# A one-layer hybrid encoder step: the softmax reciprocals of attention brought to rows by a narrow transposition and spread by two DMA queues

## Chip, cores and metric

One NeuronCore of a Trainium2 chip runs one program. The metric is the device time of one execution in microseconds, as the median of three executions. Beside these times there is one profiled execution with its trace.

## The reference

The reference computes one layer for 2048 prompt tokens and 32 sample tokens, model width 1024. An adaLN-modulated RMSNorm is followed by one wide input projection, two parallel token mixers (sparse attention and a short gated convolution), a merge by sigmoid gates, an output projection and a gated residual. The change lies in the sparse attention of the prompt. Every query keeps 256 keys that an indexer has chosen; this is the part that matters:

```python
s = jnp.einsum('bqhgd,bqkhd->bqhgk', qg, kg).astype(jnp.float32) * (HEAD_DIM ** -0.5)
s = jnp.where(valid[:, :, None, None, :], s, -jnp.inf)
p = jax.nn.softmax(s, axis=-1).astype(v.dtype)
o = jnp.einsum('bqhgk,bqkhd->bqhgd', p, vg)
...
a_out = (o * jax.nn.silu(za)) @ w_pa
```

There are 8 query heads and 2 key heads of dimension 128. Everything is float32.

## The kernel before

The program runs in stages: the normalisation and the token-wise projections with the indexer, the wide projections woven with the choice of the keys, attention, and the output projections. All products of float32 matrices are done as sums of products of split numbers: `split` (line 185) makes a rounded part `hi` on ScalarE and a rest `lo = src - hi` on another engine, by default VectorE, and three matmuls take `hi*hi`, `hi*lo` and `lo*hi`.

**Attention** (function `attention`, line 1216) handles the prompt in 16 blocks of 128 queries, in the order 4, 0, 5, 1, 6, 2, 7, 3, 8 to 15. Block `b` meets `128 * (b + 1)` keys. Each block has four pairs of heads, so there are 64 pairs. The keys that a query does not keep are masked by an additive mask, so the softmax runs over all keys of the block.

`qk(pr)` (line 1307) computes the scores of a pair's two heads, queries on partitions, into the two-bank tiles `ps` (lines 1327 to 1329). VectorE adds the mask and takes the running maximum (line 1338), ScalarE takes the exponential in place and sums it along the row (line 1342), and VectorE computes the reciprocals of the two sums (line 1343). They lie in `sc[:, 20:22]`: one number per query and head, queries on partitions. The weights in the tiles `s` stay unnormalised.

`pv(pr)` (line 1346) transposes the weights on TensorE, two key blocks and two heads at a time, into a bank `pt` (line 1363), splits them into `th` and `tl` (line 1367, in the helper's lines 186 and 187), and accumulates the weighted sum of the values in `po[:, 0:256]` (lines 1371 to 1373): the head dimension is on partitions, the queries of the two heads are along the row. Here the reciprocals are needed along the row and the same on all partitions. The kernel before makes this with matmuls:

- GpSimd rounds the reciprocals into `rr` (line 1352) and takes the rest (line 1353); it multiplies the identity by each, which gives two diagonal matrices for each of the two heads in `dg` (line 1356, two instructions);
- TensorE multiplies a matrix of ones by `dg` twice (lines 1374 and 1375), which leaves the reciprocals on all partitions of `po[:, 256:512]`, the other half of the bank;
- VectorE multiplies the gate `z`, loaded from DRAM (line 1378), by this half (line 1380), and the result by the weighted sum into `a` (line 1381).

Then GpSimd forms three sets of differences of `a` (lines 1383 to 1385), which the output projection's fast multiplication scheme uses, and SyncE stores them to `xa_d` (line 1386). The bank `po` has one buffer, `a` two, `z` three, `dg` two, `th` and `tl` five. `ptile` (line 1233) deals the banks for transpositions in turn, two from one pool and one from another.

**What sets the order.** The loop at line 1410 traces `qk` of a pair and then the `pv` of the pair three before it (`AHEAD = 3`). Between them it traces pieces of `sum_steps` (line 1147): loads, GpSimd additions (lines 376 and 1197) and stores that prepare sums of weights and conv results for the output stage, at a pace set by costs. The order on each engine is then fixed at build time by the tile framework's planner, which works on a modelled timeline (`schedule_with_timeline_sim=True`): an instruction can move ahead of an earlier traced one where the plan finds its inputs and its buffer free. At run time each engine works through its own queue in that order, and waits by semaphores.

SyncE's queue issues nearly all DMAs. GpSimd issues 16 loads of `w_g` at the start of the output stage (line 1555) and the stores of the result (line 1714), ScalarE the stores at line 781 in the first stage.

Of the kernel before, what the change touches and what calls it, by code (L numbers as in the profile page):

```python
# [9 lines left out]
F32 = mybir.dt.float32  # L10
F32R = mybir.dt.float32r
# [91 lines left out]
def body(ctx, tc, x_prompt, x_sample, cache_k, cache_v, cache_idx_k, state_conv, c_prompt, c_sample,  # L103
# [15 lines left out]
    def pad(pool, key):  # L119

        if key not in padded:
            padded.add(key)
            pool.tile([P, 16], F32, name=nm("pad"), tag=nm("pad"))
# [20 lines left out]
    s_d = dp.tile([NF, P, 1024], F32, name="s_d", tag="s_d")  # L144
    o_d = dp.tile([3, 2, 2, P, 4, 512], F32, name="o_d", tag="o_d")
# [7 lines left out]
    ones_r = cp.tile([P, P], F32R, name="ones_r")  # L153
    V.tensor_copy(ones_r, ones)
# [1061 lines left out]
    def attention(shared=None, aside=()):  # L1216
        aside = list(aside)
        sums = []
        with ExitStack() as p2:
# [59 lines left out]
            def block(b):  # L1279
# [65 lines left out]

                def pv(pr):
                    sms, sc = st.pop(pr)
                    po = pso.tile([P, 512], F32, name=nm("po"), tag="pi")
                    g = pr // 2

                    rr = ap_.tile([P, 4], F32R, name=nm("rr"), tag="rr")
                    G.tensor_copy(rr[:, 0:2], sc[:, 20:22])
                    G.tensor_tensor(rr[:, 2:4], sc[:, 20:22], rr[:, 0:2].bitcast(F32), ALU.subtract)
                    dg = ap_.tile([P, 2, 256], F32R, name=nm("dg"), tag="dg")
                    for k in range(2):
                        G.tensor_tensor(dg[:, k, :].rearrange("p (i q) -> p i q", i=2), ident.unsqueeze(1).to_broadcast([P, 2, P]),
                                        rr[:, 2 * k:2 * k + 2].bitcast(F32).unsqueeze(2).to_broadcast([P, 2, P]), ALU.mult)
# [16 lines left out]
                    T.matmul(po[:, 256:512], ones_r, dg[:, 0, :], start=True, stop=False)  # L1374
                    T.matmul(po[:, 256:512], ones_r, dg[:, 1, :], start=False, stop=True)
# [4 lines left out]
                    V.tensor_tensor(z, z, po[:, 256:512], ALU.mult)  # L1380
                    V.tensor_tensor(a[:, 0:256], z, po[:, 0:256], ALU.mult)
                    ps_ = a.rearrange("p (s t) -> p s t", s=8)
# [5 lines left out]
                return prep, [(lambda pr=pr: qk(pr), lambda pr=pr: pv(pr)) for pr in range(4)]  # L1388
# [18 lines left out]
            pend = []  # L1407
            total = sum(c for c, _ in sums)
            did = [0.0, 0.0]
            for nb, b in enumerate(order):  # L1410
# [7 lines left out]
                for qk, pv in blocks[b][1]:  # L1418
                    qk()
                    pend.append(pv)  # L1420
                    if len(pend) > AHEAD:
                        pend.pop(0)()
# [5 lines left out]
            for pv in pend:  # L1428
                pv()
# [454 lines left out]
```

## Time and profile before

| | |
|---|---|
| median of 3 executions | 2855.73 us (2851.65 to 2858.47) |
| profiled execution | 2855.3 us |
| its span, first to last instruction | 2853.4 us |
| granted TensorE clock, mean over the span | 0.994 |
| TensorE, VectorE, ScalarE, GpSimd busy | 97%, 78%, 52%, 34% |
| attention of the prompt, from its first scores to its last weighted sum | about 1780 to 2350 us |
| DMA traffic | 557.19 MB, mean 195 GB/s |

In the rows of the profile, PE is TensorE, PEld its weight loads, DVE VectorE, ACT ScalarE, POOL GpSimd and SP SyncE; a `q` behind the name marks the engine's queue, where DMAs are issued. L1375 is a line of the kernel before. A group's row ends with its busy time and the mean duration of one, and, behind a second bar, with the idle time of the engine just before these instructions and what ended it. In a row by windows, each engine has its busy time and the number of instructions; then come the granted clock, the busy share of the DMA engines and the rate. A row of waits has the total time, the number of waits and the longest. In a row of one source line, the durations are minimum, median and maximum in nanoseconds. A row of DMA issues ends with the median time from issue to landing in microseconds. Matmuls are pipelined, so two of them overlap in the trace.

### The profile page before, as it was taken

To read this page: it belongs to the slowest core of one execution; us is meant where nothing else is said; L and a number is where in the kernel's file an instruction comes from. 1 tells how busy PE (TensorE), PEld (TensorE's weight loads), DVE (VectorE), ACT (ScalarE), POOL (GpSimd) and SP (SyncE) were. 2 spreads that over 40 slices of the span, in tenths; PEclk is the share of its full clock that TensorE was granted. 3 is DMA by queue.
4 is the path that set the end of the run, shared out by engine and by line. 5 is a ranking of instruction groups with operands and counts; after the bars stand their busy time and mean duration, and the time that the engine had idled before them with its cause. 6 is when DMAs were issued, how large, how long until landed. Compare 5 with 4: busy or idle time off the path is not lost. (4 is left out here: it accounts for less than half of the span.)

```text
span 2853.4 us, 53721 instructions
## 1 busy us (share of the span) xinstructions
PE 2768.8 (97%) x18926; PEld 2674.1 (94%) x18926; DVE 2211.7 (78%) x4981; ACT 1486.7 (52%) x2861; POOL 971.3 (34%) x1440
## 2 busy tenths in 40 slices
PE   8999998999999999999999999999999999999998
PEld 6999998999999998999999999889999989999998
DVE  6666576767764778999998777878877768987988
ACT  4434334665545665655554433665655555454453
POOL 3324224545554532322323221576544430010100
PEclk9999999999999999999999999999999999999999
DMA  7425567544554546555576676576555359996785
GB/s 290 165 88 190 170 209 246 191 146 165 167 182 148 168 153 223 184 185 175 181 249 212 204 238 184 146 179 185 149 156 160 113 179 339 279 296 217 249 297 157
DMA packets 462097, 557.19 MB, mean 195 GB/s; under 512 B 171441, under 2 KB 353145, under 8 KB 460793
## 3 DMA queue, kind: packets, MB, share of 16 engines
q1 hardware_dynamic: 452952, 537.33, 59.1%
q0 software_dynamic: 4160, 12.06, 1.2%
q10 hardware_dynamic: 4704, 4.26, 0.4%
q8 instruction: 151, 2.47, 0.4%
q14 instruction: 130, 1.06, 0.1%
HBM read 369.17 MB, written 190.66 MB: 196 GB/s over the span
## 5 line engine op out<-in xcount | busy, mean ns | idle before, releaser
L991 PE MATMUL pm<-bh,wo 128*128 128x352 f32 (+1 forms) x2352 | 755.1, 323 | 6.5 <-ACT ev L1003 4.4
L992 PE MATMUL pm<-bl,wo 128*128 128x352 f32 (+1 forms) x2352 | 756.0, 322 | 0.0
L993 PE MATMUL pm<-bh,wo 128*128 128x352 f32 (+1 forms) x2352 | 754.2, 322 | 0.0
L991 PEld LDWEIGHTS pm<-bh,wo 128*128 128x128 f32 x2352 | 443.3, 189 | 15.1 <-ACT ev L1003 5.7
L992 PEld LDWEIGHTS pm<-bl,wo 128*128 128x128 f32 x2352 | 443.9, 189 | 4.8
L993 PEld LDWEIGHTS pm<-bh,wo 128*128 128x128 f32 x2352 | 442.3, 188 | 4.2 <-issue 0.2
L187 POOL TENSOR_TENSOR wo<-wr,wo 128x512 fp32r<-128x512 f32 x140 | 204.8, 1463 | 597.6 <-ACT wo L186 582.7
L759 PE MATMUL pm<-wh,hhi 128*128 128x256 f32 (+4 forms) x1088 | 307.9, 285 | 5.7 <-DVE sm L733 5.5
L760 PE MATMUL pm<-wl,hhi 128*128 128x256 f32 (+4 forms) x1088 | 307.2, 283 | 2.9 <-DVE wl L187 1.7
L761 PE MATMUL pm<-wh,hlo 128*128 128x256 f32 (+4 forms) x1088 | 305.0, 283 | 0.0
L248 DVE SCALAR_TENSOR_TENSOR sc<-pi,wi,sc 128x512 f32<-128x512 f32 (+3 forms) x287 | 192.2, 670 | 56.7 <-ACT pi L244 53.7
L186 ACT CAST th<-pt 128x512 fp32r<-128x512 f32 (+1 forms) x288 | 155.1, 561 | 137.7 <-PE pt L1363 131.1
L244 ACT ACTIVATE pi<-pi 128x512 f32<-128x512 f32 (+3 forms) x328 | 164.8, 516 | 113.1 <-PE pi L243 112.2
L1459 ACT CAST wh<-rw 128x1024 fp32r<-128x1024 f32 x128 | 134.3, 1052 | 166.0 <-PE ps L1634 81.2
L1633 PE MATMUL ps<-xh,wh 128*128 128x384 f32 (+1 forms) x672 | 214.2, 321 | 2.4 <-ACT wh L1459 0.9
L1634 PE MATMUL ps<-xl,wh 128*128 128x384 f32 (+1 forms) x672 | 214.4, 320 | 0.0
L187 DVE TENSOR_TENSOR tl<-pt,th 128x512 fp32r<-128x512 f32 (+1 forms) x288 | 183.9, 655 | 38.5 <-ACT th L186 37.3
L1635 PE MATMUL ps<-xh,wl 128*128 128x384 f32 (+1 forms) x672 | 211.7, 320 | 0.5 <-DVE wl L1460 0.5
L759 PEld LDWEIGHTS pm<-wh,hhi 128*128 128x128 f32 (+1 forms) x1088 | 198.9, 183 | 8.2 <-issue 3.5
L760 PEld LDWEIGHTS pm<-wl,hhi 128*128 128x128 f32 (+1 forms) x1088 | 199.2, 183 | 4.7 <-POOL wl L187 1.5
L761 PEld LDWEIGHTS pm<-wh,hlo 128*128 128x128 f32 (+1 forms) x1088 | 198.4, 183 | 1.0 <-DVE hlo L187 0.2
L1460 DVE TENSOR_TENSOR wl<-rw,wh 128x1024 fp32r<-128x1024 f32 x128 | 155.3, 1220 | 47.9 <-ACT wh L1459 47.7
(313 smaller groups left out, 7168.6 us busy)
## 6 DMA issues: line engine op xcount, KB each, us to landing
u<-u_d SPq DMA_DIRECT2D x112, 520.0 KB, 4.5
wr<-in_w_f_dram SPq DMA_DIRECT2D x84, 512.0 KB, 3.9
rw<-o_d SPq DMA_DIRECT2D x72, 512.0 KB, 6.8
u_d<-ev SPq DMA_DIRECT2D x168, 176.0 KB, 2.5
rw<-in_w_q_dram SPq DMA_DIRECT2D x56, 512.0 KB, 7.3
wr<-in_w_t_dram SPq DMA_DIRECT2D x32, 512.0 KB, 4.4
xa_d<-a SPq DMA_DIRECT2D x64, 256.0 KB, 3.1
s_d<-ws SPq DMA_DIRECT2D x56, 256.0 KB, 2.8
```

The lines of the kernel that those rows point to most:

```text
L187: (eng or V).tensor_tensor(lo, src, hi.bitcast(F32), ALU.subtract)
L244: S.activation(pi[:n, :w], pi[:n, :w], AF.Relu)
L248: V.scalar_tensor_tensor(sc[:n, o:o + w], pi[:n, :w], wi[:n, b, h:h + 1], sc[:n, o:o + w], ALU.mult, ALU.add)
L759: T.matmul(pm[:n, :ncol], a, hi[:, kt, :ncol], start=(kt == 0), stop=False)
L760: T.matmul(pm[:n, :ncol], a, lo[:, kt, :ncol], start=False, stop=False)
L761: T.matmul(pm[:n, :ncol], b_, hi[:, kt, :ncol], start=False, stop=(kt == KT - 1))
L991: T.matmul(ps[:, :tb], wh[:, kt, :], bh[:, kt, :tb], start=(first and kt == 0), stop=False, **more)
L992: T.matmul(ps[:, :tb], wh[:, kt, :], bl[:, kt, :tb], start=False, stop=False, **more)
L993: T.matmul(ps[:, :tb], wl[:, kt, :], bh[:, kt, :tb], start=False, stop=(kt == 3), **more)
L1633: T.matmul(ps[:, :tb], wh[:, kt, wc], xh[:, kt, :tb], start=(first and kt == 0), stop=False, **more)
L1634: T.matmul(ps[:, :tb], wh[:, kt, wc], xl[:, kt, :tb], start=False, stop=False, **more)
L1635: T.matmul(ps[:, :tb], wl[:, kt, wc], xh[:, kt, :tb], start=False, stop=(kt == 3), **more)
```

## The change

The reciprocals no longer go through diagonal matrices. A new step `spread(pr)` transposes the two columns of reciprocals on TensorE into a `pt` bank (two partitions by 128 columns), ScalarE copies them to the tile `rt` and issues, on its own queue, a DMA that writes them as 1 KB to `r_d` in DRAM. In `pv`, GpSimd issues on its queue a DMA that reads this 1 KB into all 128 partitions of `rb`. VectorE multiplies the gate by the weighted sum in the bank, directly into `a`; GpSimd multiplies `a` by `rb`. `spread` of a pair is traced after the `qk` of the pair two behind it, before the `pv` of the pair ahead of it. The matrix `ones_r`, `rr` and `dg` go; `rt` and `rb` have two buffers each, and a small pad tile stands ahead of `th`.

```diff
+    r_d = dp.tile([NB, 4, 2, P], F32, name="r_d", tag="r_d")
...
-    ones_r = cp.tile([P, P], F32R, name="ones_r")
-    V.tensor_copy(ones_r, ones)
...
+                def spread(pr):
+                    sc = st[pr][1]
+                    pt = ptile()
+                    T.transpose(pt[:2, :P], sc[:, 20:22], ident)
+                    rt = aq.tile([P, P], F32, name=nm("rt"), tag="rt")
+                    S.copy(rt[:2, :], pt[:2, :P])
+                    S.dma_start(r_d[b, pr], rt[:2, :])
+
                 def pv(pr):
-                    sms, sc = st.pop(pr)
+                    sms = st.pop(pr)[0]
                     po = pso.tile([P, 512], F32, name=nm("po"), tag="pi")
                     g = pr // 2
-
-                    rr = ap_.tile([P, 4], F32R, name=nm("rr"), tag="rr")
-                    G.tensor_copy(rr[:, 0:2], sc[:, 20:22])
-                    G.tensor_tensor(rr[:, 2:4], sc[:, 20:22], rr[:, 0:2].bitcast(F32), ALU.subtract)
-                    dg = ap_.tile([P, 2, 256], F32R, name=nm("dg"), tag="dg")
-                    for k in range(2):
-                        G.tensor_tensor(dg[:, k, :].rearrange("p (i q) -> p i q", i=2), ident.unsqueeze(1).to_broadcast([P, 2, P]),
-                                        rr[:, 2 * k:2 * k + 2].bitcast(F32).unsqueeze(2).to_broadcast([P, 2, P]), ALU.mult)
+                    pad(ap_, (id(ap_), "th"), bufs=1)
...
-                    T.matmul(po[:, 256:512], ones_r, dg[:, 0, :], start=True, stop=False)
-                    T.matmul(po[:, 256:512], ones_r, dg[:, 1, :], start=False, stop=True)
...
-                    V.tensor_tensor(z, z, po[:, 256:512], ALU.mult)
                     V.tensor_tensor(a[:, 0:256], z, po[:, 0:256], ALU.mult)
+                    rb = aq.tile([P, 256], F32, name=nm("rb"), tag="rb")
+                    G.dma_start(rb, r_d[b, pr].rearrange("(o i) q -> o (i q)", o=1).broadcast_to([P, 256]))
+                    G.tensor_tensor(a[:, 0:256], a[:, 0:256], rb, ALU.mult)
...
-                for qk, pv in blocks[b][1]:
+                for qk, spread, pv in blocks[b][1]:
                     qk()
                     pend.append(pv)
+                    rows.append(spread)
+                    if len(rows) > AHEAD - 1:
+                        rows.pop(0)()
                     if len(pend) > AHEAD:
                         pend.pop(0)()
...
+            for spread in rows:
+                spread()
             for pv in pend:
                 pv()
```

More of the change, by code (lines that the diff above doesn't have):

```diff
@@ L117, in body, with pad @@
     padded = set()
-    def pad(pool, key):
+    def pad(pool, key, **kw):
         if key not in padded:
             padded.add(key)
-            pool.tile([P, 16], F32, name=nm("pad"), tag=nm("pad"))
+            pool.tile([P, 16], F32, name=nm("pad"), tag=nm("pad"), **kw)
     cp = ctx.enter_context(tc.tile_pool(name="cp", bufs=1))
@@ L1386, in pv @@
                     store(xa_d[pr, :, :, 64 * b:64 * b + 64].rearrange("s p t -> p s t"), ps_)
-                return prep, [(lambda pr=pr: qk(pr), lambda pr=pr: pv(pr)) for pr in range(4)]
+                return prep, [(lambda pr=pr: qk(pr), lambda pr=pr: spread(pr), lambda pr=pr: pv(pr)) for pr in range(4)]
             order = [4, 0, 5, 1, 6, 2, 7, 3, 8, 9, 10, 11, 12, 13, 14, 15]
@@ L1406, in attention @@
                 v_pair(j, vst)
-            pend = []
+            pend, rows = [], []
             total = sum(c for c, _ in sums)
```

## Prediction

> **What bounds the kernel now.** I read the page first, then busy time by stretches of the attention stage, then the waits in that stage, then single instructions.
>
> ```profile
> span 2853.4 us, 53721 instructions
> PE 2768.8 (97%) x18926; PEld 2674.1 (94%) x18926; DVE 2211.7 (78%) x4981; ACT 1486.7 (52%) x2861; POOL 971.3 (34%) x1440
> ```
>
> TensorE is busy for 97% of the span, no other engine for more than 78%. That is an average over stages, so the changed stage has to be read by itself. Its first and its last pair of heads are bounded by the second ones matmul (L1375, 64 of them); the 31st shows where short pairs end.
>
> ```profile
> 1791.95 0.29 PE L1375 MATMUL po<-dg,ones_r 128*128 128x256 f32 x1
> 1956.55 0.28 PE L1375 MATMUL po<-dg,ones_r 128*128 128x256 f32 x1
> 2349.12 0.28 PE L1375 MATMUL po<-dg,ones_r 128*128 128x256 f32 x1
> ```
>
> ```profile
> core 0: us, PE busy (x) PEld busy (x) DVE busy (x) ACT busy (x) POOL busy (x), PEclk, DMA share, GB/s
> 1787.00:1945.00 158.00, 146.88 (x1045) 136.09 (x1044) 125.06 (x390) 95.68 (x217) 101.81 (x279) 0.97 0.64 162
> 1945.00:2350.00 405.00, 397.24 (x2884) 374.53 (x2884) 311.80 (x711) 234.66 (x366) 192.84 (x411) 1.00 0.54 157
> 1787.00:2350.00 563.00, 544.12 (x3927) 510.62 (x3926) 436.86 (x1101) 330.34 (x583) 294.64 (x689) 0.99 0.56 158
> ```
>
> The early stretch has short pairs: 164.6 us between the 1st and the 31st end, 30 intervals of 5.5 us. There TensorE idles 11.1 of 158 us. After 1945 us it idles 7.8 of 405 us. Over the stage it works 544.12 of 563 us, 96.6%, at a granted clock of 0.99. So an instruction less on TensorE is time off the stage, nearly in full, unless something else becomes late. What TensorE does wait for, and what was close to being late:
>
> ```profile
> PEld po L1371 <- ACT th L186: 9.6, 9, 3.6
> PE po L1371 <- DVE a L1381: 5.5, 4, 3.3
> PE po L1371 <- ACT th L186: 2.5, 3, 1.1
> DVE a L1381 <- DMA xa_d<-a: 2.7, 2, 2.5
> POOL dg L1356 <- PE po L1375: 118.6, 39, 11.4
> ```
>
> The waits on ScalarE's cast of the transposed weights sum to 12.1 us (9.6 and 2.5). Four times the next accumulation waited because VectorE had not yet read the bank, and twice VectorE itself was held because the store of tile `a` had not landed. GpSimd's 118.6 us are idle time of an engine that nobody waits for: its `dg` tile had two buffers.
>
> **TensorE.** Removed are the two ones matmuls of each pair, added is one transposition of two columns. Matmuls overlap, so their price is the distance between starts, not the duration.
>
> ```profile
> 2226.32 0.28 PE L1374 MATMUL po<-dg,ones_r 128*128 128x256 f32 x1
> 2226.44 0.28 PE L1375 MATMUL po<-dg,ones_r 128*128 128x256 f32 x1
> 2226.56 0.40 PE L1328 MATMUL ps<-klo,qh 128*128 128x512 f32 x1
> ...
> 2235.50 0.27 PE L1363 MATMUL pt<-ident,s 128*128 128x128 f32 x1
> 2235.52 0.36 PE L1371 MATMUL po<-th,vhi 128*128 128x256 f32 x1
> 2235.72 0.39 PE L1327 MATMUL ps<-khi,qh 128*128 128x512 f32 x1
> ```
>
> Two matmuls take 0.24 us, from 2226.32 to 2226.56: 64 x 0.24 = 15.4 us. A transposition alone among matmuls, with the 256-column matmul behind it, takes 0.22 us (2235.50 to 2235.72); less 0.12 us for that matmul it is 0.10 us. The narrow one streams the same 128 columns of the identity with a narrower weight load, so I take 64 x 0.10 = 6.4 us. Below, it can't be under nothing; above, its whole duration of 0.27 us would make 17.3 us and turn the term round. The spacing is the nearer row, since neighbours hide the rest. Net -9.0 us; times 96.6% for the share in which TensorE is the one that works, **-8.7 us** (bounds -14.9 and +1.8). It waits for the reciprocal of its pair, which is computed two pairs earlier, so I price that wait at nothing; without this cover it would stop every matmul queued behind it, for up to the time of a ScalarE exponential. It also takes a turn of the three banks that the transposed weights use.
>
> **ScalarE.** Added per pair: a copy of the 2x128 result, and the issue of a DMA of 1 KB. Nearest rows: a copy of 128 columns out of the bank, and the DMAs this queue issued elsewhere.
>
> ```profile
> L416 ACT COPY box<-pt x2: 266/267/268, 774.5 to 819.1; 128x128 f32<-128x128 f32 x2
> L781 ACTq DMA_DIRECT2D out_dram<-sm x17: 338/339/414, 217.3 to 462.0; - x17
> ...
> L186 ACT CAST th<-pt 128x512 fp32r<-128x512 f32 (+1 forms) x288 | 155.1, 561 | 137.7 <-PE pt L1363 131.1 <-PE po L1373 3.4 <-DVE tl L187 1.5
> ```
>
> 0.267 + 0.339 = 0.61 us, 64 times 38.8 us. ScalarE goes from 330 to 369 of 563 us. The copy waits for the transposition and the DMA for the copy; behind both stand the next casts and exponentials, and TensorE waits for casts. Scaling its 12.1 us of such waits by 369/330 gives **+1.4 us**. Ends: nothing, if all sits in ScalarE's 233 idle us, and 38.8 us, if every insertion lay ahead of a cast that TensorE awaits; that TensorE waited 12 times for 288 casts speaks for the low end.
>
> **VectorE.** Removed: one of the two multiplications that read the bank.
>
> ```profile
> L1380 DVE TENSOR_TENSOR z<-z,po 128x256 f32<-128x256 f32 x64 | 26.6, 416 | 14.3 <-PE po L1375 13.6 <-DMA xa_d<-a 0.3
> ```
>
> 26.6 us go from an engine that is not the bound. The gain is that the bank comes free 0.416 us sooner; it was waited for four times, at most 4 x 0.42 = 1.7 us. I take **-1.3 us**, since at least once the store, not this read, was late (ends 0 and -5.5).
>
> **GpSimd and the DMAs.** Removed per pair: rounding, difference, two diagonal products. Added: the issue of a DMA that reads 1 KB 128 times (128 KB), and one 128x256 product, ahead of the three differences and the store that were there.
>
> ```profile
> L1352 POOL CAST rr<-sc 128x2 fp32r<-128x2 f32 x64 | 12.0, 187 | 57.6 <-DVE sc L1343 56.7 <-DVE sc L1341 0.5
> L1353 POOL TENSOR_TENSOR rr<-sc,rr 128x2 fp32r<-128x2 f32 x64 | 12.6, 197 | 2.3
> L1356 POOL TENSOR_TENSOR dg<-ident,rr 128x256 fp32r<-128x256 f32 x128 | 76.2, 615 | 120.3 <-PE po L1375 118.6 <-DMA in<-k_d 1.7
> L1197 POOL TENSOR_TENSOR wq<-wq 128x256 f32<-128x256 f32 x96 | 72.3, 760 | 8.8 <-DMA wq<-in_w_q_dram 4.5
> L1383 POOL TENSOR_TENSOR a<-a 128x128 f32<-128x128 f32 x64 | 30.0, 469 | 58.8 <-DVE a L1381 49.1 <-DVE sc L1341 6.1 <-DVE sc L1343 3.4
> L1384 POOL TENSOR_TENSOR a<-a 128x64 f32<-128x64 f32 x64 | 21.1, 329 | 3.5
> L1385 POOL TENSOR_TENSOR a<-a 128x64 f32<-128x64 f32 x64 | 20.8, 325 | 3.7
> L1555 POOL DMA_DIRECT2D x<-in_w_g_dram x16: 548/548/824, 2352.0 to 2422.6; - x16
> z<-z_d SPq DMA_DIRECT2D x64, 128.0 KB, 2.4
> x<-in_w_g_dram POOLq DMA_DIRECT2D x16, 256.0 KB, 5.8
> xa_d<-a SPq DMA_DIRECT2D x64, 256.0 KB, 3.1
> ```
>
> Out go 0.187 + 0.197 + 2 x 0.615 = 1.61 us, in come 0.55 + 0.76 = 1.31 us: 64 x 0.30 = 19 us less work, on an engine with idle time. What matters are two new waits in its queue: the issue waits until the 1 KB has landed in DRAM, and the product until the 128 KB have landed in SBUF. Behind them stand the differences of `a`, its store, the next issue, and the additions of the weight sums, which nothing needs before the output stage. The landing lies between 2.4 us (same bytes, SyncE's queue) and 5.8 us (GpSimd's queue, twice the bytes, heavier traffic).
>
> The Trainium skill, "DMA: Bandwidth & Descriptors", section "Anatomy of one DMA — SWDGE (gpsimd) path", gives such a transfer about 2.0 us plus its bytes over 436 GB/s; by that estimate 128 KB land in 2.3 us. SyncE's 2.4 us agree with it and GpSimd's own 5.8 us do not, so the trace's ends stay; by the page the slow case below would cost nothing.
>
> The transposition is traced two weighted sums and one score product ahead of its use, over 1.5 pair times: 8 us early, 18 us later (33 intervals in 392.6 us, 11.9 us each). Against that stand 0.61 us, a landing of 1 KB (2.4 us), 0.55 us and 2.4 to 5.8 us: 6.0 to 9.4 us. So it is hidden late and about met early. The loop that can stop VectorE, and TensorE behind it, is tile `a` with two buffers: 0.42 (multiply) + 0.76 + 1.12 (differences) + 0.34 (store issue, as ScalarE's) + 3.1 (landing), 5.7 us and the hand-overs for two pairs, so 3 to 3.5 us a pair, under the mean of 5.5. Early pairs vary, so I charge **+2.0 us** (ends 0 and the slow case). The extra 64 x 128 KB = 8.4 MB stand beside 158 GB/s x 563 us = 89 MB, on DMA engines that are busy for 56%; no charge.
>
> **Sum.** -8.7 + 1.4 - 1.3 + 2.0 = -6.6 us. The profiled execution took 2855.3 us, 1.9 us more than its span, and lies 0.4 us under the median of the three runs, 2855.7. Taken from the median: **2849.1 us**. About 0.2%, 5.7 us, is what a measurement can tell from no change, so the forecast stands just past that line, at 2850.0.
>
> **Rivals.**
>
> *A, the forecast* (2841 to 2854): chance 0.62, of which 0.42 below 2850.0. Its low end is -8.7 - 5.5 us with no charge for ScalarE and GpSimd, its high end the sum with B's price.
>
> *B, ScalarE hands the gain back.* One in six insertions delays a cast that TensorE awaits: 38.8/6 = 6.5 us in place of 1.4, and the extra turn of the transposition banks holds large tiles up. Time 2849.1 + 5.1 = 2854, no change. For it: ScalarE's casts are already TensorE's largest wait. Against it: ScalarE stays at 66%. Chance 0.17.
>
> *C, slower: GpSimd's queue sets the pace of the short pairs.* The planner leaves the DMA's issue right before its product, as the code lists it. Then each pair costs GpSimd issue, landing, product and differences in series, 2.43 us plus the landing: 4.8 to 8.2 us, and 6.5 with the middle of 4.1. It decides from 5.5 us on, a landing over 3.1 us: (6.5 - 5.5) x 30 = 30 us, time 2849 + 30 = 2879; with 5.8 us, 81 us and 2930; with 3.1, nothing. For it: the `a` store already held VectorE twice. Against it: the queue orders of this trace start work when its buffer frees (`dg` was waited for 39 times behind the previous pair's matmul), so the issue should stand a pair ahead, and with two buffers the loop product, issue, landing is at most 7.1 us for two pairs, 3.6 us a pair. Chance 0.17.
>
> *D, the change does not do what it says.* The reordered stage loses in its handoffs what the matmuls gave, because the planner fills the freed places otherwise; TensorE's work falls and its idle time grows by as much. Time 2855. Chance 0.04.
>
> **How the numbers follow.** Faster by over 0.2%: 0.42, from A. Within: 0.20 of A, B and D, together 0.41. Slower: 0.17, from C. The range starts at A's low end, 2841, and ends at 2868, beyond B and D and with the part of C in which a landing takes less than 3.7 us.
>
> **What would show it.** Right: TensorE's busy time from 1787 us on falls by some 9 us with its idle time in the stage near 19 us; the narrow transpositions stand 0.10 us apart from their neighbours; ScalarE's waits by TensorE rise by less than 3 us; GpSimd's product waits for its DMA mostly before 1950 us, and VectorE's multiplication rarely for the store. B: more waits of TensorE on casts. C: GpSimd idle before the product in nearly every early pair, VectorE held by the `a` store, and TensorE by VectorE, with the early stretch longer. Wrong would be a changed stage after 1950 us, where nothing but TensorE is near its limit, or a transposition that waits for its reciprocal.

## The result, and the profile after

The changed kernel took 2878.06 us, the median of 6 runs (2874.84 to 2886.08). The kernel before, on the same chip, took 2857.41 us, also the median of 6 (2851.65 to 2858.98). The ratio is 1.0079, with a 95% interval from 1.0063 to 1.0095: slower by 0.8%, where 0.2% faster was forecast. The time lies 10 us above the predicted range.

The page of the kernel after, its first lines:

```profile
span 2874.5 us, 53369 instructions
PE 2774.6 (97%) x18862; PEld 2673.4 (93%) x18862; DVE 2194.8 (76%) x4916; ACT 1499.5 (52%) x2925; POOL 956.9 (33%) x1312
```

The span grew by 21.1 us. VectorE and GpSimd work less, as intended. TensorE has 64 instructions fewer and is busy 5.8 us longer. Busy time by stretches of the attention stage, kernel after, with the columns of the prediction's table. The prediction cut the kernel before at 1787, 1945 and 2350 us; these cuts lie at about the same work (VectorE begins to read the banks of the 1st, 31st and 64th pair into `a` at 1794.3, 1963.6 and 2368.2 us, in the kernel before at 1793.7, 1957.4 and 2350.0):

```profile
1787.00:1948.00 161.00, 144.90 (x989) 129.75 (x989) 113.10 (x351) 97.47 (x238) 92.41 (x207) 0.95 0.74 175
1948.00:2368.00 420.00, 401.29 (x2870) 375.31 (x2869) 305.71 (x680) 245.71 (x408) 189.37 (x353) 0.99 0.60 165
1787.00:2368.00 581.00, 546.19 (x3857) 505.06 (x3857) 418.81 (x1031) 343.18 (x645) 281.77 (x560) 0.98 0.64 168
```

The stage takes 581 us in place of 563, so nearly all of the loss lies in it. TensorE idles 34.8 us (581.00 less 546.19) where it idled 18.9. Most of the increase lies after 1948 us: 18.7 us idle there, against 7.8 us. What TensorE waits for, rows of its waits in the stage, kernel after:

```profile
PE po L1371 <- ACT th L185: 9.7, 6, 4.3
PE po L1372 <- DVE tl L186: 7.0, 18, 1.1
PE pt L1301 <- DMA in<-q_d: 5.5, 3, 4.4
PE pt L1363 <- ACT rt L1350: 3.4, 3, 2.3
PE pt L1348 <- DVE sc L1342: 2.6, 1, 2.6
PE po L1371 <- DVE a L1378: 0.8, 2, 0.6
```

Four things are new. Waits for ScalarE's cast `th` have a longest of 4.3 us, where it was 1.1. A load of `q` that comes late stops TensorE for up to 4.4 us, where the kernel before has this row:

```profile
PE pt L1302 <- DMA in<-q_d: 2.5, 2, 1.3
```

Waits for VectorE's cast `tl` are frequent, 18 where there were 4. And two rows belong to the new step itself: the narrow transposition (L1348) waits for its reciprocal, and the transpositions of the weights (L1363) wait for ScalarE's copy of the narrow one (L1350). One row went the hoped-for way: TensorE waits 0.8 us, not 5.5, for VectorE to read the bank.

**The two longest waits for `th`**, followed back. First TensorE, then ScalarE (two pieces of its timeline), then SyncE's queue, all of the kernel after; the bracket holds the idle time before the instruction and what ended it:

```profile
1932.69 0.58 PE L1371 MATMUL po<-th,vhi 128*128 128x256 f32 x1 [4.33 <-ACT th L185]
1989.06 0.39 PE L1371 MATMUL po<-th,vhi 128*128 128x256 f32 x1 [3.94 <-ACT th L185]
```

```profile
1930.13 0.62 ACT L185 CAST vhi<-in 128x512 fp32r<-128x512 f32 x1 [5.53 <-DMA in<-v_d]
...
1987.90 0.62 ACT L185 CAST vhi<-in 128x512 fp32r<-128x512 f32 x1 [5.59 <-DMA in<-v_d]
1988.43 1.55 ACT L185 CAST th<-pt 128x512 fp32r<-128x512 f32 x3
```

```profile
1918.05 0.46 SPq L1386 DMA_DIRECT2D xa_d<-a  x1
1924.74 0.36 SPq L1159 DMA_DIRECT2D wq<-b_d  x1
1925.15 0.46 SPq L1257 DMA_DIRECT2D in<-k_d  x1
1925.71 0.42 SPq L1257 DMA_DIRECT2D in<-v_d  x1
```

ScalarE was not busy. It stood for 5.5 us ahead of the cast of a block's new values `v`, which had not arrived, and casts of transposed weights stood behind it (three of them at 1988.43). The first of these loads of `v` was issued only at 1925.71 us, because SyncE's queue had stood, after its issue at 1918.05, until 1924.74 ahead of a load for the weight sums (L1159), whose buffer was still being stored. So a late load of a new block stops ScalarE, and ScalarE stops TensorE. The late `q` stops TensorE without ScalarE between, for 4.37 us until 1851.31.

The kernel before had such a chain once. ScalarE, VectorE and TensorE there:

```profile
1918.63 0.62 ACT L186 CAST vhi<-in 128x512 fp32r<-128x512 f32 x1 [5.86 <-DMA in<-v_d]
1919.29 0.69 DVE L187 TENSOR_TENSOR vlo<-in,vhi 128x512 fp32r<-128x512 f32 x1 [4.85 <-ACT vhi L186]
1921.38 0.35 PE L1371 MATMUL po<-th,vhi 128*128 128x256 f32 x1 [3.33 <-DVE a L1381]
```

ScalarE waited for `v`, VectorE's rest of `v` waited for ScalarE, and VectorE's two reads of the bank stood behind that rest; TensorE waited 3.33 us for the second. So a late `v` is not new in kind. New are a second one that reaches TensorE and the later `q`.

Such a stop costs twice. The windows behind the two stalls, and behind a stall of 2.44 us that ended at 2165.09, kernel after, have the granted clock as the third number from the right:

```profile
1932.00:1936.00 4.00, 3.31 (x15) 3.31 (x16) 2.47 (x6) 2.20 (x7) 1.59 (x4) 0.50 0.64 198
...
1989.00:1993.00 4.00, 3.94 (x19) 3.82 (x20) 3.77 (x11) 2.77 (x6) 0.56 (x1) 0.57 1.02 275
...
2165.00:2169.00 4.00, 3.92 (x31) 3.92 (x31) 3.86 (x9) 2.08 (x3) 0.49 (x1) 1.00 0.60 203
```

TensorE works at about half its clock for some 4 us after each of the two, by an estimate from these shares another 2 us each; behind the shorter stall the clock stays at 1.00. The Trainium skill, "TensorE: Matmul & The Clock Gate", section "Part 1: The HAM clock gate (the "warmup" mystery)", says that the clock falls to half after an idle window of about 3.4 us and that busy time of that length releases it. The traces agree for single stalls: 0.50 and 0.57 behind 4.33 and 3.94 us, 1.00 behind 2.44 us. In the kernel before, 3.33 us were enough for 0.57 from 1922 to 1926 us.

**The last pair.** TensorE, kernel after:

```profile
2335.84 0.27 PE L1348 MATMUL pt<-ident,sc 128*2 128x128 f32 x1 [2.59 <-DVE sc L1342]
2335.95 0.60 PE L1363 MATMUL pt<-ident,s 128*128 128x128 f32 x4
2338.84 1.12 PE L1363 MATMUL pt<-ident,s 128*128 128x128 f32 x4 [2.29 <-ACT rt L1350]
```

Behind the last scores, the loop's tail traces the two remaining transpositions at once, ahead of the last three weighted sums. The last one waits for its reciprocal (2.59 us), then the next transpositions wait for ScalarE to have emptied its bank (2.29 us): both behind an exponential over all 2048 keys. From 2340 to 2344 us the granted clock is 0.50 here as well, though neither stall is longer than 2.59 us: two short ones with only five transpositions between them were enough.

### The profile page after: what moved, and what is told of

Read it like the earlier page. It is cut to its first block, busy times and chain, and to the rows that moved or that the text cites. A ratio compares the mean times of both kernels' runs of the same rounds, so it can differ in the third digit from the quotient of the medians.

```text
span 2874.5 us, 53369 instructions
## 1 busy us (share of the span) xinstructions
PE 2774.6 (97%) x18862; PEld 2673.4 (93%) x18862; DVE 2194.8 (76%) x4916; ACT 1499.5 (52%) x2925; POOL 956.9 (33%) x1312
## 3 DMA queue, kind: packets, MB, share of 16 engines
q10 hardware_dynamic: 4960, 4.33, 0.4%
## 4 chain that ended last, share of the span: by engine, by line
PE 66%; DVE 17%; DMA 8%; issue 4%; ACT 3%; POOL 1%; SPq 1%; DVEq 0%; ACTq 0%; POOLq 0%
PE pm L990 8%; PE pm L991 8%; PE pm L992 8%; PE pt L1363 3%; PE pm L759 3%; PE pm L758 3%; PE pm L760 3%; PE ps L1638 2%; PE ps L1639 2%; PE ps L1640 2%; PE po L1372 2%; DMA rw<-in_w_q_dram 2%; PE ps L1326 2%; PE po L1373 2%; PE po L1371 2%
```

## The experiments

Each time is the median of its runs, in microseconds, with the ratio to the kernel before on the same chip; that kernel took 2853 to 2857 us in every series. Line numbers are those of the kernel after. The theories, in the order in which they stood:

- *T1*: what is new on GpSimd holds the loop of tile `a` and through it SyncE's queue, and with it the loads of q, k and v.
- *T2*: waits of the new step have no cover at the last pair.
- *T3*: the planner made a worse order, and none of the added work costs anything by itself.
- *T4*, formed later: the narrow transposition's turn of the three banks is what costs.

| kernel | time | ratio, 95% interval |
|---|---|---|
| after | 2878.1 | 1.0079 [1.0063, 1.0095] |
| no_product | 2878.9 | 1.0092 [1.0071, 1.0113] |
| no_spread | 2856.2 | 1.0009 [0.9997, 1.0021] |
| z_pool | 2899.6 | 1.0158 [1.0137, 1.0178] |
| store_pool | 2868.7 | 1.0058 [1.0037, 1.0078] |
| tail_late | 2867.2 | 1.0055 [1.0036, 1.0074] |
| qkv_act | 2865.4 | 1.0044 [1.0027, 1.0061] |
| qkv_act_before | 2854.3 | 1.0002 [0.9992, 1.0012] |
| tail_qkv | 2859.2 | 1.0021 [1.0010, 1.0032] |
| spread_dve | 2894.7 | 1.0143 [1.0126, 1.0160] |
| before_replan | 2856.8 | 1.0009 [0.9999, 1.0019] |
| rows_dma | 3128.4 | 1.0959 [1.0941, 1.0978] |
| floor | 2838.7 | 0.9958 [0.9939, 0.9976] |
| floor_rows | 2869.2 | 1.0039 [1.0024, 1.0053] |
| floor_rows_qkv | 2852.8 | 1.0003 [0.9991, 1.0015] |
| floor_turn | 2864.3 | 1.0050 [1.0033, 1.0067] |
| floor_rb | 2864.1 | 1.0031 [1.0015, 1.0048] |
| bank_half | 2869.3 | 1.0042 [1.0029, 1.0055] |
| bank_qkv | 2868.9 | 1.0044 [1.0030, 1.0058] |

**Which part costs: product, spread, or the place of the product.** Four kernels, each with one part of the change taken out or moved.

*no_product* drops GpSimd's multiplication.

```diff
-                    G.tensor_tensor(a[:, 0:256], a[:, 0:256], rb, ALU.mult)
```

> The changed kernel without GpSimd's product of a and rb; the rows are still transposed, copied, written and spread, so attention's output stays unnormalised. Before 2857, changed 2878. Theory 1 (the product stands between VectorE's multiplication and the store of a; SyncE's queue waits for that store with the loads of v and q behind it, ScalarE then stands in the cast of v and TensorE idles): the store comes about 0.8 us a pair sooner, SyncE's wait for GpSimd's last difference falls from 87 to about 40 us, time 2855 to 2862. Theory 2 (the spread itself costs: a transposition bank, ScalarE's copy and issue, GpSimd's issue behind the 1 KB write): stays at 2872 to 2880. Theory 3 (no part costs; the planner's new order put the loads of v late by chance): anywhere from 2855 to 2885, without a relation to the part removed.

*no_spread* drops transposition, copy and both DMAs; the product stays, with a constant.

```diff
-                    rows.append(spread)
-                    if len(rows) > AHEAD - 1:
-                        rows.pop(0)()
...
-                    G.dma_start(rb, r_d[b, pr].rearrange("(o i) q -> o (i q)", o=1).broadcast_to([P, 256]))
-                    G.tensor_tensor(a[:, 0:256], a[:, 0:256], rb, ALU.mult)
+                    G.tensor_tensor(a[:, 0:256], a[:, 0:256], ones_w, ALU.mult)
```

> The changed kernel without transposition, copy, 1 KB write and broadcast; GpSimd multiplies a by a constant tile of ones, so the output stays unnormalised. Theory 1: the product still delays the store, 2866 to 2874 (TensorE saves the 6 us of narrow transpositions). Theory 2: 2842 to 2850, that is before less the 15 us of ones matmuls and some stalls. Theory 3: anywhere from 2845 to 2880.

*z_pool* lets GpSimd multiply the gate `z` ahead of the bank instead of `a` behind it.

```diff
+                    G.tensor_tensor(z, z, rb, ALU.mult)
                     a = aq.tile([P, 512], F32, name=nm("a"), tag="a", bufs=2)
                     V.tensor_tensor(a[:, 0:256], z, po[:, 0:256], ALU.mult)
-                    G.tensor_tensor(a[:, 0:256], a[:, 0:256], rb, ALU.mult)
```

> GpSimd multiplies the gate z by rb before the bank is ready, instead of a by rb after it; the result is the same in exact terms and nothing is left out. Theory 1: the tail from the bank to the store is the one of before, 2850 to 2860. Theory 2: 2872 to 2880, as all of the spread is still there. Theory 3: no relation, 2855 to 2885.

*store_pool* issues the store of `a` on GpSimd's queue, so that SyncE's queue never stands for `a`.

```diff
-                    store(xa_d[pr, :, :, 64 * b:64 * b + 64].rearrange("s p t -> p s t"), ps_)
+                    G.dma_start(xa_d[pr, :, :, 64 * b:64 * b + 64].rearrange("s p t -> p s t"), ps_)
```

> The changed kernel with the store of a issued by GpSimd's own queue, behind the differences, instead of SyncE's. Theory 1: SyncE's queue no longer waits for GpSimd, the loads of v are issued in time, 2850 to 2862; GpSimd pays 64 x 0.59 us for the issues, 38 us of an engine that idles. Theory 2: 2872 to 2885. Theory 3: no relation, 2855 to 2885.

Measured: 2878.9, 2856.2, 2899.6 and 2868.7. The first fits T2; the second and the fourth lie between the ranges of T1 and T2, the third above all. Without the product nothing is gained, so T1 in its first form, the product as the cause, falls. Without the spread the whole loss is gone. Moving the product ahead of the bank is worse; the trace has TensorE waiting 18.8 us for `th`, once for 8.1 us, again behind a late `v` (ScalarE waits up to 10.3 us for one). Taking the stores out of SyncE's queue helps, by 9 us (6 by the ratios); a late `q` stops TensorE there too, once for 7.0 us. What GpSimd's product waits for in the kernel after:

```profile
POOL a L1381 <- DVE a L1378: 219.9, 49, 17.5
```

The product waits for VectorE's `a`, 49 times, and none of its waits is ended by the landing of `rb`. The landing (median 3.7 us) was in time, since the issue stands a pair ahead (at 2092.28 us, for instance, for the product at 2109.97).

**Late loads, and the last pair.** *qkv_act* issues the loads of q, k and v on ScalarE's queue, and *qkv_act_before* does the same in the kernel before, as a control. *tail_late* changes only the loop's tail.

```diff
-                load(t.rearrange("p (j c) -> p j c", j=2), d[j * P:(j + 2) * P, :].rearrange("(j p) c -> p j c", p=P))
+                S.dma_start(t.rearrange("p (j c) -> p j c", j=2), d[j * P:(j + 2) * P, :].rearrange("(j p) c -> p j c", p=P))
...
-                            load(q, q_d[r0:r0 + P, 512 * g:512 * g + 512])
+                            S.dma_start(q, q_d[r0:r0 + P, 512 * g:512 * g + 512])
```

> The changed kernel, nothing left out; the loads of q, k and v for the next block are issued by ScalarE's queue instead of SyncE's. Theory 1 in its second form (after the first four runs: not the product, but SyncE's queue as a whole holds these loads behind sums and stores that became later; TensorE's stalls of about 4 us at the starts of blocks are late q, k or v): the stalls of 4.4, 4.3 and 3.9 us at 1851, 1933 and 1989 us go, with the clock loss behind them, 2858 to 2866. Theory 2 (ScalarE's insertions): ScalarE gets 36 more issues of 0.34 us, 2876 to 2885. Theory 3: 2860 to 2885, stalls of the same kind in other places.

> Control: the kernel before with the loads of q, k and v on ScalarE's queue. Theory 1b (late loads are something that the change brought): the kernel before has few such stalls, 2850 to 2858. If moving them is worth as much without the change: 2840 to 2846.

```diff
-            for spread in rows:
-                spread()
-            for pv in pend:
+            for i, pv in enumerate(pend):
+                if i < len(rows):
+                    rows[i]()
                 pv()
```

> The changed kernel, nothing left out; only the last two transpositions of rows move: each is traced ahead of one of the last weighted sums instead of both at once behind the last scores. In the changed kernel's trace TensorE waits there 2.6 us for a reciprocal, 2.3 us for the copy out of the bank and 0.9 us for a cast, and its clock then falls to 0.5 for 4 us. Theory 1 (queue and loads): these are a small part, time 2870 to 2874. Theory 2 (each part of the spread costs where its wait is uncovered): the same 4 to 7 us, with the wait for the reciprocal gone. Theory 3 (plan by chance): 2865 to 2885, waits elsewhere moved too.

*tail_qkv* is both edits in one.

> The changed kernel, nothing left out, with both earlier edits: loads of q, k and v by ScalarE's queue, and the last two transpositions one at a time. Each alone gave 11 to 13 us. Theory 1b and 2 (two separate places): they add up, 2853 to 2858. Theory 3: they do not add up, 2858 to 2872.

Measured: 2865.4, 2854.3, 2867.2 and 2859.2. The same move of the loads that gains 13 us after the change gains nothing before it, so what it gains is a loss that the change made. The waits of TensorE in qkv_act and in tail_late that answer to the rows above, one fence each:

```profile
PE pt L1301 <- DMA in<-q_d: 7.1, 4, 4.7
PE po L1372 <- DVE tl L186: 6.2, 18, 1.1
PE pt L1363 <- ACT rt L1350: 3.1, 2, 2.4
PE po L1371 <- ACT th L185: 2.9, 5, 0.9
PE pt L1348 <- DVE sc L1342: 2.6, 1, 2.6
```

```profile
PE po L1372 <- DVE tl L186: 7.7, 19, 1.5
PE po L1371 <- ACT th L185: 6.5, 5, 2.9
PE pt L1363 <- ACT rt L1350: 1.1, 2, 0.8
```

In qkv_act the waits for `th` are back at 2.9 us, and the two waits of the tail are still there. ScalarE's two waits for `v` of 5.5 and 5.6 us are 2.1 and 1.6 us. The late `q` is not cured: it stops TensorE for 4.7 us here and for 4.9 us in tail_qkv. In tail_late the wait for the reciprocal is gone. Until 2327 us every engine's queue stands there in the same order as in the changed kernel, so only the tail differs; the lower wait for `th` is what one execution differs from another, and the profiled one took 2857.7, 9.5 us under the median.

By the ratios the two edits gain 0.35% and 0.24%, and together 0.58%: they add up. By the medians they gain 12.7 us, as T1 gave it, and 10.9, which is more than the 4 to 7 us that T1 and T2 gave, and together 18.8: 2859.2 lies just past the range for adding up and inside that of T3. T2 is shown, as its edit touches the tail alone. T1 in the form "loads late behind SyncE's queue" has edit, control and waits for it where `v` is concerned. But the planner gave every other engine another order as well, so how much of the gain is the queue alone is not shown. What stays above the kernel before is 0.2%, with the late `q` in it. The waits for `tl` stay in both.

**Other carriers for the step.** *spread_dve* gives the copy to VectorE and the write of 1 KB to GpSimd's queue, *rows_dma* drops transposition and copy and lets a DMA write the reciprocals from their columns to DRAM, 256 elements of 4 bytes.

```diff
-                    S.copy(rt[:2, :], pt[:2, :P])
-                    S.dma_start(r_d[b, pr], rt[:2, :])
+                    V.tensor_copy(rt[:2, :], pt[:2, :P])
+                    G.dma_start(r_d[b, pr], rt[:2, :])
```

> The changed kernel, nothing left out; VectorE instead of ScalarE copies the two rows out of the bank, and GpSimd's queue instead of ScalarE's writes them to DRAM, so ScalarE is as loaded as before. Theory 1: stalls at the starts of blocks stay, 2870 to 2880. Theory 2 (ScalarE's insertions delay casts: TensorE's waits for the rest tl rose from 8 to 19 us): these waits fall back to about 8 us, 2864 to 2872. Theory 3: 2860 to 2885.

```diff
-                    pt = ptile()
-                    T.transpose(pt[:2, :P], sc[:, 20:22], ident)
-                    rt = aq.tile([P, P], F32, name=nm("rt"), tag="rt")
-                    S.copy(rt[:2, :], pt[:2, :P])
-                    S.dma_start(r_d[b, pr], rt[:2, :])
+                    S.dma_start(r_d[b, pr].rearrange("i q -> q i"), sc[:, 20:22])
```

> The changed kernel, nothing left out, but the two columns of reciprocals go to DRAM directly, by a DMA on ScalarE's queue that writes 256 numbers of 4 bytes: no narrow transposition, no turn of a transposition bank, no copy by ScalarE. TensorE's waits for the rest tl were about 12 us in every run with the narrow transposition, also where ScalarE did not copy, and 5 to 6 us in those without. Theory 2b (the transposition's turn of a bank and its waits cost, not the DMAs): these waits fall to 5 to 6 us, the 5 to 6 us at the last pair go, and 6 us of transpositions; 2855 to 2862. Theory 1b (the DMAs and the later stores hold up SyncE's queue and late q, k, v loads remain): 2866 to 2874. Theory 3 (plan by chance): 2850 to 2885 with stalls of q, k, v loads in other places.

Measured: 2894.7 and 3128.4, both above every range. The first has the waits for `tl` no lower (7.2 us), so nothing speaks for the load on ScalarE as their cause; VectorE, which makes `tl`, has the copy instead. Its late loads are worse: TensorE waits 13.3 us for `q`, ScalarE 20.8 us for `v`. The second is worse by far: the DMA of small elements goes with slower transfers beside it, as the last section shows.

**What the removed work was worth, and another traced order.** *floor* is the kernel before without anything that spreads the reciprocals. *before_replan* is the kernel before with the same instructions in another traced order.

```diff
-                    rr = ap_.tile([P, 4], F32R, name=nm("rr"), tag="rr")
...
-                    T.matmul(po[:, 256:512], ones_r, dg[:, 0, :], start=True, stop=False)
-                    T.matmul(po[:, 256:512], ones_r, dg[:, 1, :], start=False, stop=True)
...
-                    V.tensor_tensor(z, z, po[:, 256:512], ALU.mult)
```

> The kernel before without rr, dg, the two ones matmuls and VectorE's multiplication by them, so attention's output stays unnormalised; nothing is put in their place. It shows what the removed work is worth. If TensorE's work sets the stage, as the prediction had it, 64 x 0.24 us = 15 us go and it takes 2838 to 2842. If loads and hand-overs set part of the stage, as in the run with a constant rb (2856), 2848 to 2858.

In before_replan the lines that make `rr` and `dg` move from ahead of the loop over key blocks to behind it.

> Control: the kernel before with GpSimd's rr and dg traced behind the weighted sums instead of ahead of them; the same instructions, nothing left out. Theory 3 (a new plan alone moves the time by ten microseconds and more): outside 2849 to 2860. Theories 1 and 2: inside it, as the ones matmuls were covered.

Measured: 2838.7 and 2856.8. Removal alone is worth 15.4 us by the medians, 12 by the ratio. before_replan does not test T3: its trace has the instructions of the stage in the same order as the kernel before, on every engine, so the planner made the same plan, and the 0.1% (an interval that holds zero) says only how well a time repeats. The nearest to a test is qkv_act_before, where the planner did give every engine another order: 2854.3, no change. One such order is no proof, and T3 stays open for what the planner's order costs in any of these kernels.

**The transposition by itself.** *floor_rows* puts only the narrow transposition and ScalarE's copy on floor; *floor_turn* only the transposition; *floor_rows_qkv* is floor_rows with the loads of q, k and v on ScalarE's queue; *floor_rb* puts only GpSimd's DMA on floor. The tail of the kernels with the transposition is that of tail_late.

```diff
+                def spread(pr):
+                    sc = st[pr][1]
+                    pt = ptile()
+                    T.transpose(pt[:2, :P], sc[:, 20:22], ident)
+                    rt = aq.tile([P, P], F32, name=nm("rt"), tag="rt")
+                    S.copy(rt[:2, :], pt[:2, :P])
```

> floor (the kernel before without reciprocal work, its output left unnormalised) with the narrow transposition and ScalarE's copy added, no DMA, no product. The prediction's price: 2838.7 plus 6.4 for the transpositions and about 1 for ScalarE, 2846. If the bank turn is what costs: TensorE's waits for tl go from 4.2 and 6.4 us to some 7 and 12, and the time to 2850 or more.

floor_turn lacks the last two of these lines.

> floor_rows without ScalarE's copy: only the narrow transposition, which takes its turn of the three banks and is read by nobody (output left unnormalised). Theory that the bank, held until ScalarE has copied, is what costs: 2845 to 2847 (floor's 2838.7 plus 64 x 0.11 us of transpositions), with TensorE's waits for tl back at 4 and 6 us. Theory that the turn itself, or the shifted order of the queues, costs: 2855 or more, with late v loads as in floor_rows.

> floor_rows (2869.2: narrow transposition and ScalarE's copy on the kernel without reciprocal work; output left unnormalised) with the loads of q, k and v issued on ScalarE's queue. Theory late loads: ScalarE's casts of v no longer stand for 4.5 and 5.7 us waiting for v at block starts; the time falls by 10 to 16 us, to 2853 to 2859, with some 7 us of TensorE's own work for the transpositions and 5 us of waits for tl left above floor's 2838.7. Theory the copy itself is what stalls: no change, 2866 to 2870.

```diff
                     V.tensor_tensor(a[:, 0:256], z, po[:, 0:256], ALU.mult)
+                    rb = aq.tile([P, 256], F32, name=nm("rb"), tag="rb")
+                    G.dma_start(rb, r_d[b, pr].rearrange("(o i) q -> o (i q)", o=1).broadcast_to([P, 256]))
```

> floor with GpSimd's queue issuing the DMA that spreads a constant kilobyte over 128 partitions for each pair, and nothing else (no transposition, no copy, no product; output left unnormalised). The prediction charged the 8.4 MB nothing: 2838 to 2840. If the DMA traffic or the issue alone makes the q, k and v loads late: stalls of 4 us at block starts, 2845 to 2852.

Measured: 2869.2, 2864.3, 2852.8 and 2864.1. The last lies above both of its ranges. Transposition and copy, with no DMA and no product, cost 30 us on floor (27 by the means of the runs). Without the copy it is still 26 (24). With the loads on another queue it is 14 (13). So more than half goes with the place of these loads, now with nothing new on GpSimd at all. ScalarE's waits for `v` in floor and in floor_turn, one fence each (in floor_rows they are 17.6 us, the longest 5.7):

```profile
ACT vhi L186 <- DMA in<-v_d: 11.1, 5, 3.3
```

```profile
ACT vhi L186 <- DMA in<-v_d: 20.0, 5, 5.8
```

The longest grows from 3.3 to 5.8 us by one transposition per pair that nobody reads. What is left in floor_rows_qkv, 14 us, has no wait for `v` over 2.3 us. It has a stall of 4.2 us for a late `q`, but floor has one too (4.9 us), so that one needs no part of the spread. TensorE's waits for `tl` in floor, and below in floor_rows_qkv:

```profile
PE po L1366 <- DVE tl L187: 4.2, 6, 1.5
```

```profile
PE po L1373 <- DVE tl L187: 6.8, 18, 1.5
```

The waits are three times as many and short. floor_rb was not the clean price that it was meant to be: with no reader of `rb`, the planner let GpSimd's queue run its issues between the differences of `a`, where they wait for earlier landings. GpSimd's, VectorE's and TensorE's rows of that run:

```profile
POOL rb L1376 <- DMA rb<-r_d: 50.7, 38, 3.4
...
DVE a L1374 <- DMA xa_d<-a: 13.5, 10, 2.1
...
PE po L1367 <- DVE a L1374: 17.6, 10, 4.8
```

That is much like the chain of the prediction's rival C: GpSimd stands for a landing, the store of `a` goes out late, VectorE waits for it, TensorE for VectorE. In the changed kernel it did not occur.

**The bank's turn.** *bank_half* puts the narrow transposition of the next pair into the free half of `po`, where the ones matmuls wrote before, so that it takes no turn of the three banks. *bank_qkv* has the loads on ScalarE's queue as well.

```diff
-                    pt = ptile()
+                    pt = ptile() if po is None else po[:, 256:512]
                     T.transpose(pt[:2, :P], sc[:, 20:22], ident)
...
                     po = pso.tile([P, 512], F32, name=nm("po"), tag="pi")
...
+                    if nxt is not None and not late:
+                        nxt(po)
...
```

> The changed kernel with the narrow transposition of the next pair put into the free half of the accumulation bank (where the ones matmuls wrote before), so that it takes no turn of the three banks of the transposed weights; at the last pair it stands behind the accumulation. Theory bank turn: TensorE's waits for VectorE's cast tl fall from 7.0 and 12.0 us to the 3.0 and 4.9 of before, some 11 us, and the waits at the last pair go as well, up to 10 us: 2857 to 2867. Theory other (the turn costs nothing, the spread's DMAs do): only the last pair's waits go, 2867, with the tl waits unchanged.

> The same, with the loads of q, k and v issued on ScalarE's queue as in tail_qkv. Theory bank turn: 2859.2 of tail_qkv less some 5 to 9 us: 2850 to 2854, at or below the kernel before. Theory other: 2859, as tail_qkv.

Measured: 2869.3 and 2868.9. bank_half lies past the upper end that T4 gave (2867) and beside the other theory's number, so by time T4 is not borne out. The waits say more. TensorE, bank_half:

```profile
PE po L1373 <- ACT rt L1350: 10.7, 8, 5.6
PE po L1348 <- DVE a L1382: 4.9, 5, 3.5
PE po L1374 <- DVE tl L186: 0.8, 1, 0.8
```

The waits for `tl` at the accumulation fell from 7.0 to 0.8 us, which fits a cause in the turn of the banks. It is not proof: the accumulation now waits for ScalarE's copy, 10.7 us, and a wait for `tl` can lie hidden under that one; no_product and store_pool keep the turn and wait only 4.4 and 4.7 us for `tl`. bank_qkv is 10 us worse than tail_qkv, above both expectations: a wait was exchanged for a dearer one. No version that leaves nothing out beat the kernel before.

## Why the prediction was wrong, point by point

The runs form a ladder, each step one part, by the medians: floor 2838.7; with transposition and copy, and the loads on ScalarE's queue (floor_rows_qkv), 2852.8; with both DMAs and the product (tail_qkv) 2859.2; with the loads back on SyncE's queue and the uncovered tail (after) 2878.1. That is +14, +6 and +19 us on a removal worth 15. The rungs come from different series, so each step is good to 2 or 3 us, and each also carries the order that the planner found for it.

- *Removing the ones matmuls*, priced at 64 x 0.24 = 15.4 us: right, as far as floor's own order of the queues allows. floor gained 15.4 us by the medians (0.4%, interval 0.24% to 0.61%), and that includes VectorE's multiplication and GpSimd's diagonals, which the prediction also held to be worth little.
- *The narrow transposition*, priced at 0.10 us between neighbours: right as a spacing, wrong as a cost. TensorE around one of them in the kernel after:

```profile
2225.82 0.28 PE L1373 MATMUL po<-th,vlo 128*128 128x256 f32 x1
2225.94 0.27 PE L1348 MATMUL pt<-ident,sc 128*2 128x128 f32 x1
2225.97 0.36 PE L1371 MATMUL po<-th,vhi 128*128 128x256 f32 x1
2226.17 0.28 PE L1372 MATMUL po<-tl,vhi 128*128 128x256 f32 x1
```

  From 2225.94 to 2226.17 pass 0.23 us, of which the 256-column matmul has 0.12: 0.11 us for the narrow one, 7 us for 64. But with ScalarE's copy, and with no late `v` (the late `q` stays), it cost 14 us. The prediction mentioned that the transposition "takes a turn of the three banks" and gave this no price in the sum; only rival B named it, with 5.1 us for it and ScalarE's insertions together. The more frequent waits for `tl` are what the traces show of it. How much of the 14 us is the turn and how much is ScalarE's insertion was not separated.
- *"It waits for the reciprocal of its pair, which is computed two pairs earlier, so I price that wait at nothing"*: this step failed at the last pair, where nothing is computed in between. The wait is 2.59 us, and 2.29 us follow behind it, as the prediction's own condition said ("without this cover it would stop every matmul queued behind it"). With the slowed clock it is worth 7 to 11 us (tail_late).
- *ScalarE's insertions*, +1.4 us: their durations were 0.255 and 0.230 us, less than the 0.267 and 0.339 assumed. The term failed all the same: it scaled TensorE's 12.1 us of waits for the cast `th` by ScalarE's load, to 13.5 us, and they became 22.8 us (9.7 and 13.1). The large ones were ScalarE's own waits for `v`, not its load. spread_dve, which takes copy and issue off ScalarE, was slower.
- *VectorE's earlier release of the bank*, -1.3 us: the waits fell further, from 5.5 to 0.8 us, but the reading was wrong. The longest, 3.33 us, was neither the second read of the bank nor the store of `a`, but the late `v` at 1918.63 us; in the changed kernel such stops come by way of ScalarE's casts. That this row fell by more than forecast is luck.
- *GpSimd and the DMAs*, +2.0 us: right in kind. Issue 0.587 us, landing 3.7 us, product 0.737 us, all in time; product and DMAs together are some 6 us of the ladder. Rival C, which was the forecast's only slower case, gave 2879 us and hit the measured time by luck: its mechanism did not occur in the changed kernel.
- *SyncE's queue* is the step that was missing, and the largest. The prediction asked of each moved instruction what it would be queued behind on GpSimd and ScalarE. It did not ask what was late, or nearly late, in the queue that the change does not touch, and the one stop of this kind in the kernel before it put down to VectorE. ScalarE's waits for the loads of `v` went from 10.0 us in four to 18.2 us in five, the longest from 5.9 to 5.6; what grew is how many reach TensorE, from one of 3.33 us to two of 4.33 and 3.94. With the `q` at 1851.31 us that makes 12.6 us of stalls in place of 4.5 (3.33, and 1.15 for `q`), and the slowed clock behind them. One transposition per pair that nobody reads was enough for late loads of `v` of that size (floor_turn). qkv_act with its control gives 10 to 13 us of the loss to the queue of these loads, under the reservation made there.
- *"Wrong would be a changed stage after 1950 us ... or a transposition that waits for its reciprocal"*: both came. TensorE's busy time from 1787 us on was to fall by some 9 us; it rose by 3.2, from 1031.1 to 1034.3, in part because matmuls take longer behind a stall (0.41 us in place of 0.28 for 256 columns).

What stays open: why the loads of `v` and `q` come later in these kernels. That they stand behind those of the weight sums in SyncE's queue is not it by itself, for so they do in the kernel before (a load of the weight sums at 2047.30 us, `v` at 2048.00). Nothing was tried here beyond moving loads and stores to other queues. Also open is why the product alone costs 17 us between floor and no_spread, while its removal from the changed kernel saves nothing. SyncE's queue may be the reason: from floor to no_spread its waits for the store of `a` rise from 33.7 to 73.9 us, while without the product, from after to no_product, they only move, from the store (84.3 to 42.0) to the load of `z` behind VectorE's `a` (77.6 to 114.1). That is argued from these sums, not shown by a run.

## What to carry to other kernels

When the engine that bounds the kernel is 97% busy, its own price list gives the gain, but the loss can come from whatever else is nearly late: before a change, list the waits for loads that are already close, in every queue, and ask which of them a shift of a few microseconds would uncover. Follow the longest wait back by more than one step; here the engine that it named was itself waiting for a load. Before a reordered kernel counts as a control, look whether its trace has another order at all. A step that is covered by running two pairs ahead has no cover at the end of the loop, so price the last trip by itself. And an operation squeezed between others on an idle-looking resource also takes a buffer turn there, which can have a price of its own.

## What the runs showed of the hardware

A DMA that gathers single elements is dear beyond its own bytes. In rows_dma the write of 1 KB in 256 elements of 4 bytes took 9.8 us to land (median). The transfers beside it slowed down; the first 563 us of the stage in that run, where it lasts beyond 2600 us:

```profile
1787.00:2350.00 563.00, 370.86 (x2272) 343.17 (x2272) 258.21 (x716) 206.96 (x396) 192.80 (x413) 0.81 0.71 109
```

The DMA engines are busier than in the same window of the kernel before (0.71 against 0.56) and of the changed kernel (0.65), and move less, 109 GB/s in place of 158 and 172; the store of `a` lands in 5.6 us where it took 3.1 in the kernel before.

A read of 1 KB into 128 partitions, issued on GpSimd's queue, landed in 3.7 us (the median of 64; the longest 7.3) with 0.587 us of GpSimd's time. The Trainium skill, "DMA: Bandwidth & Descriptors", section "Anatomy of one DMA — SWDGE (gpsimd) path", would make it 2.3 us by an estimate from its fit; the trace does not agree under this traffic of 168 GB/s, and the median lies within the bounds of 2.4 to 5.8 us that the prediction took from its own rows.
